# A hybrid decoder step: means of rows formed behind a half's first job, loads reordered, and weights times values in three passes of halves

## The chip, the cores and the metric

The kernel runs on one NeuronCore of a Trainium2 chip. The metric is the device time of one execution in microseconds (us); several executions are timed, and one is recorded by the hardware profiler. TensorE (PE) multiplies matrices, VectorE (DVE) and ScalarE (ACT) do elementwise work, GpSimd (POOL) helps, SyncE (SP) issues most DMAs. Each engine works off its own instructions in order and waits on semaphores for the others.

## The reference

One layer over T = 1104 token columns: 16 meta tokens and 1024 prompt tokens (causal), and 8 sequences of 8 sample tokens with 1024 cached positions each. The width is 1024, everything is float32.

```
x += 0.5 * rmsnorm(swiglu(rmsnorm(x, g1), Wg, Wu, Wd), g1p)        # FFN 1, hidden width 2816
h  = rmsnorm(x, gm); q, k, v, B, C, hc = split(h @ w_in)           # mixer
A  = softmax(q1 k1^T / 8) - lam * softmax(q2 k2^T / 8)             # 4 heads, two maps each
o  = rmsnorm(A @ v, subln) * (1 - lambda_init);  c = B * conv3(C * hc)
x += rmsnorm(concat(o, c) @ w_out, gp)
x += 0.5 * rmsnorm(swiglu(rmsnorm(x, g2), ...), g2p)               # FFN 2
rmsnorm(x, g) = x * rsqrt(mean(x * x) + eps) * g                   # mean over the 1024 features of a token
```

## The kernel before

Features lie on the 128 partitions, tokens in the columns. The 1104 columns are two **halves** p = 0, 1 of 552, each of two groups g of 276; a matmul takes 276 columns. Nearly every matrix product is made of float32r operands: each operand is split into a high part (ACT copies it, L175) and a low part (DVE subtracts, L176; the helper is `halves`), and `three` (L169 to L171) issues three passes, high x high, high x low, low x high.

The stages follow one another: `phase` for FFN 1's gate and up products, `down` for its down product, `phase` for w_in, attention, `down` for w_out, `phase` for FFN 2, `down` at the end.

**A phase.** Most of its weight units are done by `seven`: a unit is a 2 x 2 block product made with seven products instead of eight, of the operand's combinations that `quarters(p)` prepares (44 DVE operations and 28 ACT copies a half) and of the weights' combinations that `weights_piece(0..6)` prepares (DVE and ACT). Preparing takes time, so the first two or three jobs (unit u, half p) of a phase are **plain**: full float32 matmuls (L296) straight from the normalized rows in Y, 32 matmuls recorded as 64, over 8 chunks c of 128 features. Job (0,0) goes chunk by chunk with four PSUM banks, the others go group by group. `weights_of` loads a unit's raw weights into WR; one further unit per phase is copied early into a DRAM tile (`early`) and loaded from there into the end of W (`late_raw`).

**Between stages.** `down` sums tiles (q, dd, g) into Y, adds their squares into R (`sq_add`), and at the end of a half runs a background generator, `junction(p)`: `ready` forms the mean over features (`mean_r`: a matmul with a matrix of 1/1024, L204, then `rsqrt` on ACT and DVE), then per chunk multiplies by R and a gain (L543), adds the residual (L546) and stores the chunk; `heads` squares the chunk for the next norm into the tile ss2 (L218, L221, L222) and scales it by the next gain (L266), and after the last chunk it calls `mean_r` for the next norm; then `quarters`. For half 1 that is done in two parts, group 0 and group 1. The first layer's input goes through `heads` directly. A `Background` object steps through these generators between matmul jobs; `need(("h", p))` steps until that half's heads are done, the mean included, before a plain job of that half is written.

**Attention.** For each of 4 heads and 9 row blocks qi: `scores` (L929, float32r), `weights` (softmax and difference), `flip`: transposes of up to four 128 x 128 blocks into the one PSUM bank "fl" (L967), a copy to the tile "at" by DVE (L969) or ACT (L970) in turn, then the products with the values, one full float32 matmul per block (L982, recorded as two), and `sub_norm`. The sample sequences' work is spread between. Constants (identity, masks) lie in WR.

**Order.** `in_turn` writes a PE instruction behind the last one; a planner places everything else on each engine by its own simulated times, within the dependencies. `tc.issue_after(x)` puts what is written in it behind x on x's engine. `dma` issues from SP, `keep` from POOL.

Of the kernel before, what the change touches and what calls it, by code (L numbers as in the profile page):

```python
# [9 lines left out]
F32R = mybir.dt.float32r  # L10
# [5 lines left out]
P = 128  # L16
# [27 lines left out]
def hybrid_step(ctx: ExitStack, tc: tile.TileContext, ins, outs, n_pool):  # L44
# [104 lines left out]

    last_pe, last_dma = [None], [None]  # L150

# [104 lines left out]

    def heads(p, ready, gain, parts=((0, 1),)):


        ss2 = temp("ss2", HT)  # L260
        for gs in parts:
            t = slice(gs[0] * G, gs[-1] * G + G)
            for n, c in enumerate(ready(gs)):
                x = lay["yv"][p][:, c, :]
                sq_add(ss2, x, n == 0, gs)
                act.activation(x[:, t], x[:, t], AF.Copy, scale=gains[:, gain, c:c + 1])  # L266
                yield
            yield
            mean_r(lay["R"][p], ss2, gs)
            yield  # L270

    class Background:
# [15 lines left out]
    def plain(u, p, raw, use, outer, step):  # L288
# [11 lines left out]
        if outer:  # L300
            banks.update({(n, g): bank("mm")[:, :G] for g in range(2) for n in range(2)})
            for n, c in enumerate(PAIR_K):
                in_turn(part, [c], range(2))
                if n:
                    step()
                    if n > 2:
                        step()
            for g in range(2):
                use.plain(g, banks[0, g], banks[1, g])
        else:  # L310
            for g in range(2):
                banks.update({(n, g): bank("mm")[:, :G] for n in range(2)})
                for i in range(0, 8, 2):
                    in_turn(part, PAIR_K[i:i + 2], [g])
                    step()
                use.plain(g, banks[0, g], banks[1, g])

    def weights_of(src):
        dma(wraw, src)

    def weights_piece(n):
# [24 lines left out]
    def phase(n, src, early, late, uses, background, loaded=False, tail=iter(())):  # L346
# [6 lines left out]
        if not loaded:  # L353
            weights_of(src(1 - late))
        dma(late_raw, early)
        for u, p in [(0, 0), (0, 1), (1, 0)][:2 + late]:
            background.need(("h", p))
            if p and not late:
                for m in range(5):
                    weights_piece(m)  # L360
            plain(u, p, raws[u], uses(u, p), p == 0 and u == 0, background.step)
        if late:
            seven([(2, 0), (2, 1), (1, 1)] + [(u, p) for u in range(3, n) for p in range(2)], src, uses, background,
                  tail=tail)
        else:
            seven([(u, p) for u in range(1, n) for p in range(2)], src, uses, background, 5, tail)
# [110 lines left out]

    def down(src, blocks, base, order, place, w_src, reuse, g_post, g_pre, res, dst):

# [10 lines left out]
        inputs = [(p, b, i) for p in range(2) for b in range(nb) for i in range(blocks[b])]  # L490
        wt, raws, put = {}, [], []

# [19 lines left out]
        def load_input():  # L512
            p, b, i = inputs.pop(0)
            slot = xs[p][:, base(b) + i]
            dma(f32(slot[:, 0, :]), src(b, i, p))
            put.append(slot)

# [38 lines left out]
        def begin():  # L556
# [82 lines left out]
    for c in PAIR_K:  # L639
        dma(lay["yv"][1][:, c, :], ins["x1"][:, c, :])  # L640
    background = Background((("h", 0), heads(0, lambda gs: entering(0), G_F1PRE)),
                            (("h", 1), heads(1, lambda gs: entering(1), G_F1PRE)),
                            (("x", 0), quarters(0)), (("x", 1), quarters(1)))
# [178 lines left out]
    Q = [ring("q0", 4, TP, F32R), None]  # L822
    vs = ring("vs0", 1, 1152)
    qs_t, = ring("qs", 1, 1024)
# [12 lines left out]
    Q[1] = ring("q1", 4, TP, F32R)  # L837
    vbuf = [v.rearrange("p (j e) -> p j e", j=9) for v in vs + ring("vs1", 1, 1152)]
    pbuf = ring("p", 6, TP)
    abuf = [a.rearrange("p (j q) -> p j q", j=9) for a in ring("at", 4, 1152)]  # L840
    tq = ring("t", 10, 256)
    onesV, = ring("onesV", 1, P)
    cst = WR[:, 1470:]
    gp.memset(onesV, 1.0 / DV)
# [6 lines left out]

    dma(cst, ins["consts"])

# [8 lines left out]
    def load_v(h):  # L862
        dma(vbuf[h % 2][:, 0:8, :], v_spill[h, :, 0:8, :])
        dma(vbuf[h % 2][:N_META, 8, :], v_spill[h, :N_META, 8, :])
# [5 lines left out]
    load_v(0)  # L870
    for n in range(2):
        split_qk(0, n)

    def mixer_constants():
# [33 lines left out]
    def prompt_jobs(h):  # L908
# [50 lines left out]
        def flip(aw, qi):  # L959
            rows = N_META if qi == 0 else P  # L960
            at = of(abuf, "at")
            for j0 in range(0, qi + 1, 4):
                js = range(j0, min(j0 + 4, qi + 1))
                ps = bank("fl")
                for j in js:
                    kr = N_META if j == qi else P
                    nc.tensor.transpose(ps[:kr, (j - j0) * P:(j - j0) * P + rows], aw[:rows, j * P:j * P + kr],  # L967
                                        ident[:rows, :rows])
                copy = lambda dst, src: (dve.tensor_copy(dst, src) if (qi + j0 // 4) % 2  # L969
                                         else act.activation(dst, src, AF.Copy))  # L970
                n = len(js) - (js[-1] == qi)
                if n:
                    copy(at[:, j0:j0 + n, :rows], ps[:, :n * P].rearrange("p (j q) -> p j q", q=P)[:, :, :rows])
                if js[-1] == qi:
                    copy(at[:N_META, qi, :rows], ps[:N_META, n * P:n * P + rows])
            if qi < 1 or qi % 2 == 0:
# [139 lines left out]
    for step, job in enumerate(jobs):  # L1116
        nxt = step // 9 + 1
        if nxt < H:
# [21 lines left out]
    def place(p, b, q):  # L1140
        if q == 0:
# [3 lines left out]
    begin, run = down(both, (4, 4), lambda b: 4 * b, lambda p, b: (1, 2, 3, 0) if p and not b else (0, 1, 2, 3), place,  # L1145
                      lambda b, q: ins["w_out"][b, q], True, G_MPOST, G_F2PRE, x_spill, x_mid)
    for _ in begin:
# [94 lines left out]
```

## Time and profile before

| | us |
|---|---|
| median of 3 timed runs | 2297.01 (2293.79 to 2299.85) |
| the profiled execution | 2293.83 |
| its span | 2292.1 |
| PE busy | 2136.1 (93%) |
| DVE busy | 1404.7 (61%) |
| ACT busy | 929.5 (41%) |
| POOL busy | 299.8 (13%) |
| PE waiting for a mean's squares (L204 for ss) | 77.0 in 6 waits |

The profiled execution is 1.7 us longer than its span, and near the lowest of the timed runs. A busy engine is one with an instruction in flight; a matmul's record is longer than its spacing to the next one, so PE also counts as busy in short pauses. "Granted clock" is the share of TensorE's full 2.4 GHz that the chip gave; it has two levels, 1 and 0.5. The stages, by their times in the span: FFN 1 until about 802, w_in until 1106, attention until 1346, w_out until 1482, FFN 2 until the end.

### The profile page before, as it was taken

What the parts mean: (1) busy time and instruction counts of PE and PEld (TensorE: products, weight loads), DVE (VectorE), ACT (ScalarE), POOL (GpSimd) and SP (SyncE); (2) the same over time, 40 slices, a digit from 0 to 9 for tenths busy, and PEclk for the clock granted to TensorE, in tenths of its full rate; (3) what the DMA queues carried; (4) which work ended last, traced back from release to release, by engine and by line L of the source; (5) the groups of instructions that cost most, each with busy time, mean ns of one, the idle gap of its engine ahead of it and who ended that gap; (6) DMA issues with size and microseconds to landing.
All of it is one profiled execution on the core that took longest, in us unless ns stands there. A gap on an engine that the chain in (4) does not pass through costs nothing.

```text
span 2292.1 us, 41517 instructions
## 1 busy us (share of the span) xinstructions
PE 2136.1 (93%) x16126; PEld 2038.4 (89%) x16126; DVE 1404.7 (61%) x2973; ACT 929.5 (41%) x1960; POOL 299.8 (13%) x419
## 2 busy tenths in 40 slices
PE   6899999999999979999799978749999999999997
PEld 5799999999999959999667768739999999999997
DVE  5766556655567775466457656765665665645756
ACT  7433333334254442333235555553333333332522
POOL 0111111110000004443302110001111111100000
PEclk9899999999999989999789889879999999999998
DMA  7121222235444313321567332112122222543443
GB/s 276 55 81 67 81 81 68 81 116 197 130 144 142 131 51 120 124 86 60 191 206 274 125 137 102 67 35 78 67 81 81 68 80 81 175 144 127 141 148 98
DMA packets 115240, 263.48 MB, mean 115 GB/s; under 512 B 14514, under 2 KB 56114, under 8 KB 107602
## 3 DMA queue, kind: packets, MB, share of 16 engines
q1 hardware_dynamic: 109698, 244.92, 31.7%
q0 software_dynamic: 5344, 15.90, 1.9%
q8 instruction: 126, 2.06, 0.4%
q14 instruction: 72, 0.59, 0.1%
HBM read 206.47 MB, written 61.97 MB: 117 GB/s over the span
## 4 chain that ended last, share of the span: by engine, by line
PE 51%; issue 31%; DVE 7%; POOL 5%; DMA 3%; ACT 2%; SPq 1%; POOLq 0%; ACTq 0%; DVEq 0%
PE mm L169 13%; PE mm L170 13%; PE mm L171 13%; POOL u L440 3%; POOL n L440 3%; PE po L982 2%; PE mm L296 2%; PE qk L929 2%; DVE X L176 2%; PE fl L967 1%; PE sa L1059 1%; PE st L204 1%; PE sa L1024 1%; DVE Y L546 1%; DVE Y L543 1%
## 5 line engine op out<-in xcount | busy, mean ns | idle before, releaser
L169 PE MATMUL mm<-X,W 128*128 128x276 f32 x3868 | 1130.1, 292 | 27.8 <-ACT W L175 10.5
L170 PE MATMUL mm<-X,W 128*128 128x276 f32 x3868 | 1127.2, 291 | 2.8 <-DVE X L176 2.8
L171 PE MATMUL mm<-X,W 128*128 128x276 f32 x3868 | 1126.6, 291 | 1.9 <-DVE W L176 1.9
L169 PEld LDWEIGHTS mm<-X,W 128*128 128x128 f32 x3868 | 732.0, 189 | 31.0 <-ACT W L175 11.4
L170 PEld LDWEIGHTS mm<-X,W 128*128 128x128 f32 x3868 | 733.0, 190 | 4.3 <-DVE X L176 4.0
L171 PEld LDWEIGHTS mm<-X,W 128*128 128x128 f32 x3868 | 733.3, 190 | 3.2 <-DVE W L176 3.2
L176 DVE TENSOR_TENSOR W<-WR,W 128x512 fp32r<-128x512 f32 (+3 forms) x421 | 329.1, 793 | 116.4 <-ACT W L175 114.8
L175 ACT ACTIVATE W<-WR 128x512 fp32r<-128x512 f32 (+3 forms) x421 | 284.1, 689 | 249.6 <-PE mm L170 134.8
L420 ACT ACTIVATE n<-mm 128x276 f32<-128x276 f32 x210 | 84.2, 401 | 317.5 <-PE mm L171 299.0
L586 DVE TENSOR_TENSOR Y<-Y,mm 128x276 f32<-128x276 f32 x288 | 126.3, 439 | 128.1 <-PE mm L171 123.4
L440 POOL TENSOR_TENSOR u<-u,R 128x276 f32<-128x276 f32 x93 | 75.1, 807 | 493.2 <-ACT u L471 265.3
L440 POOL TENSOR_TENSOR n<-n,R 128x276 f32<-128x276 f32 x83 | 65.4, 787 | 547.2 <-ACT n L449 547.2
L170 PE MATMUL mm<-X 128*128 128x276 f32 x416 | 121.9, 293 | 2.7 <-DVE X L176 2.7
L169 PE MATMUL mm<-X 128*128 128x276 f32 x416 | 123.0, 296 | 1.5 <-ACT X L175 1.5
L423 DVE TENSOR_TENSOR n<-mm,n 128x276 f32<-128x276 f32 x105 | 46.8, 445 | 125.7 <-PE mm L171 113.9
L171 PE MATMUL mm<-X 128*128 128x276 f32 x416 | 121.4, 292 | 0.0
L221 ACT ACTIVATE sq<-Y 128x276 f32<-128x276 f32 x168 | 68.2, 428 | 86.4 <-DVE Y L586 58.7
L176 DVE TENSOR_TENSOR X<-X 128x552 fp32r<-128x552 f32 x104 | 75.5, 728 | 38.4 <-ACT X L175 37.9
L169 PE MATMUL mm<-X,X 128*128 128x276 f32 x320 | 93.9, 293 | 0.0
L170 PE MATMUL mm<-X,X 128*128 128x276 f32 x320 | 93.1, 291 | 0.0
L171 PE MATMUL mm<-X,X 128*128 128x276 f32 x320 | 93.1, 291 | 0.0
L929 PE MATMUL qk<-q,q 64*128 64x336 f32 (+10 forms) x360 | 69.9, 385 | 15.5 <-ACT q L175 11.1
(174 smaller groups left out, 2669.3 us busy)
## 6 DMA issues: line engine op xcount, KB each, us to landing
WR<-in_w_gu SPq DMA_DIRECT2D x43, 1024.0 KB, 4.8
WR<-in_w_dn SPq DMA_DIRECT2D x48, 640.0 KB, 3.9
X<-hid SPq DMA_DIRECT2D x88, 276.0 KB, 4.1
kp<-in_cache_k SPq DMA_DIRECT2D x64, 256.0 KB, 3.9
vp<-in_cache_v SPq DMA_DIRECT2D x64, 256.0 KB, 4.4
hid<-u SPq DMA_DIRECT2D x93, 138.0 KB, 1.8
hid<-n SPq DMA_DIRECT2D x83, 138.0 KB, 1.7
WR<-in_w_in SPq DMA_DIRECT2D x11, 1024.0 KB, 4.9
```

The lines of the kernel that those rows point to most:

```text
L169: nc.tensor.matmul(ps, lh, rh, start=first, stop=False, **kw)
L170: nc.tensor.matmul(ps, lh, rl, start=False, stop=False, **kw)
L171: last_pe[0] = nc.tensor.matmul(ps, ll, rh, start=False, stop=last, **kw).ins
L175: tc.keep_in_program_order(act.activation(hi, raw, AF.Copy))
L176: on.tensor_tensor(lo, raw, f32(hi), op=ALU.subtract)
L221: act.activation(sq, src[:, s], AF.Square)
L296: last_pe[0] = nc.tensor.matmul(banks[n, g], w, lay["yv"][p][:, c, g * G:g * G + G], start=c == PAIR_K[0], stop=c == PAIR_K[-1]).ins
L420: act.activation(t, ps, AF.Copy)
L423: dve.tensor_tensor(self.n1, ps, self.n1, op=ALU.add)
L440: on.tensor_tensor(t, t, lay["R"][p][:, g * G:g * G + G], op=ALU.mult)
L586: dve.tensor_tensor(y, y, ps, op=ALU.add)
L929: last_pe[0] = nc.tensor.matmul(pw[m], a[r, q0:q0 + P], b[r, k0:k1], start=n == 0, stop=n == 2, tile_position=(m * DH, 0)).ins
```

## The change

1. `heads` no longer calls `mean_r`, and yields twice less per part; it leaves its sums in `sums_of[p]`. A new `rms(p, gs)` forms that mean. `plain` calls it after the job's matmuls and before their results are used: for job (0,0) after all of them, for the others after each group. For half 0 of a `down`, `rms(0, (0, 1))` stands after tile 7 of half 1's last block. For the first input the sums are kept in R itself.
2. In the last block of half 1 the junction of half 1 steps from tile 9 on (tile 8 before), twice at tile 15; in w_out the junction of half 0 steps 8 times in block 0 (10 before).
3. A plain job steps its background only until what the next job needs is done (`upto`).
4. In FFN 1 the third plain job is written behind the load and the first five pieces of the next unit's weights; they were prepared after it. The load of `early` is written behind the last load noted in `last_load`.
5. `down` for w_out gets its first weight tile ready made (`have`): loaded in attention's step 4, split in step 12. Its inputs are split before its other weights.
6. In attention V is split into halves (`split_v`), the transposed weights are copied to a high part by ACT, the low part is subtracted by DVE, and `three` does the products. The constants get a tile of their own (cst) instead of a part of WR, loaded after the first V.

```diff
+    sums_of = {}
+    def rms(p, gs):
+        if p in sums_of:
+            mean_r(lay["R"][p], sums_of[p], gs)
+            if gs[-1]:
+                del sums_of[p]
-    def heads(p, ready, gain, parts=((0, 1),)):
-        ss2 = temp("ss2", HT)
+    def heads(p, ready, gain, parts=((0, 1),), at_r=False):
+        ss2 = sums_of[p] = lay["R"][p] if at_r else temp("ss2", HT)
...
                 yield
-            yield
-            mean_r(lay["R"][p], ss2, gs)
-            yield
...
+        def upto(self, name):
+            return lambda: self.step() if any(n == name for n, _ in self.named) else None
...
                     if n > 2:
                         step()
+            rms(p, (0, 1))
             for g in range(2):
                 use.plain(g, banks[0, g], banks[1, g])
...
                     step()
+                rms(p, (g,))
                 use.plain(g, banks[0, g], banks[1, g])
...
-        dma(late_raw, early)
-        for u, p in [(0, 0), (0, 1), (1, 0)][:2 + late]:
+        with tc.issue_after(last_load[0]):
+            dma(late_raw, early)
+        jobs = [(0, 0), (0, 1), (1, 0)][:2 + late]
+        for u, p in jobs:
             background.need(("h", p))
-            if p and not late:
+            if (u, p) == jobs[-1]:
+                if late:
+                    weights_of(src(2))
                 for m in range(5):
                     weights_piece(m)
-            plain(u, p, raws[u], uses(u, p), p == 0 and u == 0, background.step)
+            last = ("x", 1) if (u, p) == jobs[-1] else ("x", 0) if p else ("h", 1)
+            plain(u, p, raws[u], uses(u, p), p == 0 and u == 0, background.upto(last))
...
-            for n in range(max(blocks[0], 3)):
-                if n < 3:
+            if have:
+                for n in range(blocks[0]):
+                    split_input()
+            for n in range(3):
+                if n or not have:
                     split_item()
                     load_item()
-                if n < blocks[0]:
+                if not have:
                     split_input()
...
-                        if n % 4 == 3 if nb > 2 else n % 2 if b else n < 10:
+                        if n % 4 == 3 if nb > 2 else n % 2 if b else n < 8:
                             first.step()
-                        if p and b == nb - 1 and g:
+                        if p and b == nb - 1 and n > 8:
                             second.step()
+                            if n == 15:
+                                second.step()
                         if p and b == nb - 1 and n == 7:
+                            rms(0, (0, 1))
                             second = Background(*junction(1))
...
-    cst = WR[:, 1470:]
+    cst, = ring("cst", 1, K_W)
...
+    def split_v(h):
+        lo, hi = vbuf[h % 2]
+        halves(hi[:, 0:8, :], lo[:, 0:8, :], f32(lo[:, 0:8, :]), dve)
+        halves(hi[:N_META, 8, :], lo[:N_META, 8, :], f32(lo[:N_META, 8, :]), dve)
...
-                copy = lambda dst, src: (dve.tensor_copy(dst, src) if (qi + j0 // 4) % 2
-                                         else act.activation(dst, src, AF.Copy))
...
+                for src, r, j in parts:
+                    act.activation(hi[r, j, :rows], src, AF.Copy)
+                    dve.tensor_tensor(lo[r, j, :rows], src, f32(hi[r, j, :rows]), op=ALU.subtract)
...
-                nc.tensor.matmul(po[:, off:off + rows], vt_[:kr, j, :], at[:kr, j, :rows], start=j == 0, stop=j == qi)
+                three(po[:, off:off + rows], vt_[1][:kr, j, :], vt_[0][:kr, j, :], hi[:kr, j, :rows], lo[:kr, j, :rows],
+                      j == 0, j == qi)
...
+            if step % 9 == 7:
+                split_v(nxt)
+        if step == 4:
+            dma(WR[:, :1024], ins["w_out"][0, 0])
+        if step == 12:
+            w = W[:, 1024:2048], W[:, 0:1024]
+            halves(w[0], w[1], WR[:, :1024], dve)
+            first_w = {(0, 0, 0): (w[1], w[0])}
```

## Rows read from the trace of the kernel before

**Rows 1.** Page, part 1: each engine's busy us, share of the span, instructions.
```profile
PE 2136.1 (93%) x16126; PEld 2038.4 (89%) x16126; DVE 1404.7 (61%) x2973; ACT 929.5 (41%) x1960; POOL 299.8 (13%) x419
```

**Rows 2.** Waits of PE: who waited for whom, total us, times, longest.
```profile
PE st L204 <- DVE ss L222: 77.0, 6, 24.0
```

**Rows 3.** Timeline of PE: start, us, instructions, idle before and releaser.
```profile
17.39 2.18 PE L204 MATMUL st<-ss,onesD 128*128 128x276 f32 x4 [17.39 <-DVE ss L222]
...
74.75 0.60 PE L169 MATMUL mm<-X,W 128*128 128x276 f32 x1 [7.66 <-ACT W L175]
...
837.70 1.29 PE L204 MATMUL st<-ss,onesD 128*128 128x276 f32 x2 [11.18 <-DVE ss L222]
...
865.04 0.60 PE L169 MATMUL mm<-X,W 128*128 128x276 f32 x1 [6.25 <-ACT n L420]
...
1117.28 0.94 PE L929 MATMUL qk<-q,q 64*128 64x336 f32 x3 [11.09 <-ACT q L175]
...
1355.01 0.60 PE L169 MATMUL mm<-X,W 128*128 128x276 f32 x1 [8.60 <-ACT X L175]
...
1439.04 2.21 PE L204 MATMUL st<-ss,onesD 128*128 128x276 f32 x4 [12.72 <-DVE ss L222]
...
1530.80 1.29 PE L204 MATMUL st<-ss,onesD 128*128 128x276 f32 x2 [24.00 <-DVE ss L222]
```

**Rows 4.** Windows around the stage changes: us, each engine's busy time, clock, DMA.
```profile
18.00:39.00 21.00, 21.00 (x80) 16.76 (x79) 8.89 (x22) 17.99 (x40) 0.21 (x1) 1.00 1.02 350
39.00:87.00 48.00, 38.23 (x168) 31.86 (x167) 44.69 (x109) 26.49 (x72) 6.44 (x6) 0.86 0.16 57
795.00:866.00 71.00, 48.38 (x222) 40.03 (x222) 52.42 (x128) 34.43 (x84) 4.53 (x8) 0.84 0.14 49
1426.00:1441.00 15.00, 2.28 (x8) 1.60 (x6) 11.02 (x21) 8.80 (x20) 0.00 (x0) 0.62 0.21 79
1441.00:1552.00 111.00, 76.82 (x428) 68.63 (x427) 75.75 (x192) 60.50 (x145) 3.09 (x4) 0.82 0.14 47
```

**Rows 5.** Timeline of PE: a whole plain job of half 1, before w_in.
```profile
838.78 16.93 PE L296 MATMUL mm<-Y,W 128*128 128x276 f32 x64
```

**Rows 6.** Timelines of DVE and ACT before w_in's units.
```profile
811.05 0.44 DVE L222 TENSOR_TENSOR R<-R,sq 128x276 f32<-128x276 f32 x1
...
863.57 1.13 ACT L175 ACTIVATE W<-WR 128x512 fp32r<-128x512 f32 x2
864.61 0.67 ACT L420 ACTIVATE n<-mm 128x276 f32<-128x276 f32 x2
```

**Rows 7.** SP's issues and a window at attention's two ends.
```profile
1106.22 0.33 SPq L153 DMA_DIRECT2D W<-early_w  x1
...
1344.26 6.05 SPq L153 DMA_DIRECT2D WR<-in_w_out  x2
1350.41 1.79 SPq L153 DMA_DIRECT2D X<-c_spill  x4
...
1108.00:1116.00 8.00, 0.00 (x0) 0.00 (x0) 0.00 (x0) 1.00 (x1) 0.86 (x2) 0.55 0.94 341
```

**Rows 8.** Attention: a window, runs of matmuls, durations (min/median/max), DVE's copies.
```profile
1180.00:1346.00 166.00, 162.36 (x1340) 116.15 (x1340) 110.92 (x423) 89.34 (x237) 33.39 (x48) 0.95 0.52 173
...
1229.36 1.06 PE L982 MATMUL po<-at,vs 128*128 128x128 f32 x8
...
L982 PE MATMUL po<-at,vs x360: 257/275/579, 1137.1 to 1345.2; 128*128 128x128 f32 x144, 16*128 16x128 f32 x32, 16*128 16x16 f32 x4
...
1245.75 2.14 PE L1046 MATMUL sa<-s_comb,s_p 128*128 128x64 f32 x18
...
1228.88 0.44 PE L929 MATMUL qk<-q,q 64*128 64x144 f32 x2
...
L969 DVE COPY at<-fl 128x512 f32<-128x512 f32 x12 | 8.2, 683 | 0.4 <-PE fl L967 0.4
```

**Rows 9.** Timeline of PE: the last mean of the run.
```profile
2278.94 0.73 PE L204 MATMUL st<-R,onesD 128*128 128x276 f32 x2 [2.02 <-DVE R L222]
```

More of the change, by code (lines that the diff above doesn't have):

```diff
@@ L319, in weights_of @@
         dma(wraw, src)
+        last_load[0] = last_dma[0]
     def weights_piece(n):
@@ L354, in phase @@
             weights_of(src(1 - late))
-        dma(late_raw, early)
-        for u, p in [(0, 0), (0, 1), (1, 0)][:2 + late]:
+        with tc.issue_after(last_load[0]):
+            dma(late_raw, early)
+        jobs = [(0, 0), (0, 1), (1, 0)][:2 + late]
+        for u, p in jobs:
             background.need(("h", p))
-            if p and not late:
+            if (u, p) == jobs[-1]:
+                if late:
+                    weights_of(src(2))
                 for m in range(5):
                     weights_piece(m)
-            plain(u, p, raws[u], uses(u, p), p == 0 and u == 0, background.step)
+            last = ("x", 1) if (u, p) == jobs[-1] else ("x", 0) if p else ("h", 1)
+            plain(u, p, raws[u], uses(u, p), p == 0 and u == 0, background.upto(last))
         if late:
-            seven([(2, 0), (2, 1), (1, 1)] + [(u, p) for u in range(3, n) for p in range(2)], src, uses, background,
-                  tail=tail)
+            seven([(2, 0), (2, 1), (1, 1)] + [(u, p) for u in range(3, n) for p in range(2)], src, uses, background, 5,
+                  tail)
         else:
@@ L475, in plain, with down @@
             self.put(t, g)
-    def down(src, blocks, base, order, place, w_src, reuse, g_post, g_pre, res, dst):
+    def down(src, blocks, base, order, place, w_src, reuse, g_post, g_pre, res, dst, have=()):
         X, xs, yv, R = lay["X"], lay["xs"], lay["yv"], lay["R"]
@@ L490, in down @@
         inputs = [(p, b, i) for p in range(2) for b in range(nb) for i in range(blocks[b])]
-        wt, raws, put = {}, [], []
+        wt, raws, put = dict(have), [], []
+        loads = [n for n in loads if n not in wt]
         def key(p, b, q):
@@ L515, in load_input @@
             dma(f32(slot[:, 0, :]), src(b, i, p))
+            last_load[0] = last_dma[0]
             put.append(slot)
@@ L822, in hybrid_step @@
     Q = [ring("q0", 4, TP, F32R), None]
-    vs = ring("vs0", 1, 1152)
+    vs = ring("vs0", 1, 1152, F32R)
     qs_t, = ring("qs", 1, 1024)
@@ L837, in hybrid_step @@
     Q[1] = ring("q1", 4, TP, F32R)
-    vbuf = [v.rearrange("p (j e) -> p j e", j=9) for v in vs + ring("vs1", 1, 1152)]
+    vbuf = [[v.rearrange("p (j e) -> p j e", j=9) for v in (lo, hi)]
+            for lo, hi in (vs + ring("vh0", 1, 1152, F32R), ring("vs1", 2, 1152, F32R))]
+    cst, = ring("cst", 1, K_W)
     pbuf = ring("p", 6, TP)
-    abuf = [a.rearrange("p (j q) -> p j q", j=9) for a in ring("at", 4, 1152)]
+    abuf = [[a.rearrange("p (j q) -> p j q", j=9) for a in ring(f"at{n}", 2, 1152, F32R)] for n in range(2)]
     tq = ring("t", 10, 256)
     onesV, = ring("onesV", 1, P)
-    cst = WR[:, 1470:]
     gp.memset(onesV, 1.0 / DV)
@@ L862, in load_v @@
     def load_v(h):
[L863 to L864 removed]
+        lo = f32(vbuf[h % 2][0])
+        dma(lo[:, 0:8, :], v_spill[h, :, 0:8, :])
+        dma(lo[:N_META, 8, :], v_spill[h, :N_META, 8, :])
+    def split_v(h):
+        lo, hi = vbuf[h % 2]
+        halves(hi[:, 0:8, :], lo[:, 0:8, :], f32(lo[:, 0:8, :]), dve)
+        halves(hi[:N_META, 8, :], lo[:N_META, 8, :], f32(lo[:N_META, 8, :]), dve)
     load_qk(0)
@@ L870, in hybrid_step @@
     load_v(0)
+    dma(cst, ins["consts"])
     for n in range(2):
         split_qk(0, n)
+    split_v(0)
     def mixer_constants():
@@ L968, in flip @@
                                         ident[:rows, :rows])
-                copy = lambda dst, src: (dve.tensor_copy(dst, src) if (qi + j0 // 4) % 2
-                                         else act.activation(dst, src, AF.Copy))
                 n = len(js) - (js[-1] == qi)
+                parts = []
                 if n:
-                    copy(at[:, j0:j0 + n, :rows], ps[:, :n * P].rearrange("p (j q) -> p j q", q=P)[:, :, :rows])
+                    parts.append((ps[:, :n * P].rearrange("p (j q) -> p j q", q=P)[:, :, :rows], slice(0, P), slice(j0, j0 + n)))
                 if js[-1] == qi:
-                    copy(at[:N_META, qi, :rows], ps[:N_META, n * P:n * P + rows])
+                    parts.append((ps[:N_META, n * P:n * P + rows], slice(0, N_META), qi))
+                for src, r, j in parts:
+                    act.activation(hi[r, j, :rows], src, AF.Copy)
+                    dve.tensor_tensor(lo[r, j, :rows], src, f32(hi[r, j, :rows]), op=ALU.subtract)
             if qi < 1 or qi % 2 == 0:
@@ L1145, in hybrid_step @@
     begin, run = down(both, (4, 4), lambda b: 4 * b, lambda p, b: (1, 2, 3, 0) if p and not b else (0, 1, 2, 3), place,
-                      lambda b, q: ins["w_out"][b, q], True, G_MPOST, G_F2PRE, x_spill, x_mid)
+                      lambda b, q: ins["w_out"][b, q], True, G_MPOST, G_F2PRE, x_spill, x_mid, first_w)
     for _ in begin:
```

9 lines of the change are left out of this document (4 added, 5 removed).

## The prediction

> **What bounds the kernel now.** I read the page's busy shares first: TensorE is busy 93% of the span, VectorE 61%, ScalarE 41% [rows 1]. So the time is TensorE's work plus the places where it stands still, and the second view is who it waits for. One wait stands out: the mean's matmul (L204) waits for the squares' sum ss, 77.0 us in 6 waits [rows 2]. The third view, TensorE's timeline, shows where: 17.39 us at the start, 11.18 (and a smaller one) before w_in, 12.72 and 24.00 (and a smaller one) between w_out and FFN 2; beside them stand other pauses of 6 to 11 us at the same stage changes and at attention's two ends [rows 3]. The reader is to see that all of it lies at stage changes. There I asked for windows, to see what else could be late: VectorE is busy 8.89 of 21 us in the first stall, then 44.69 of 48 (93%); 52.42 of 71 (74%) before w_in; 11.02 of 15 and 75.75 of 111 (together 69%) before FFN 2 [rows 4]. So a wait taken from TensorE can be won back only as far as VectorE's own work there can be packed tighter. I use one rule for that: VectorE packs to 85%, halfway from the poorer windows to the 93% that the saturated one reaches; the bounds are no better than now (nothing won) and 92%.
>
> **Mean behind the job.** The mean's matmul stands in TensorE's order ahead of the plain job and holds it until the last chunk's square is added. After the change the job's 64 matmuls (16.93 us [rows 5]) stand ahead of the mean and need only their own chunk. The mean itself costs the same. What is late next is VectorE: behind the plain jobs come `seven`'s products, which need the quarters of half 1 and the weights' pieces. The trace shows that chain already: ScalarE's copy of a product (L420 at 864.61) stands behind the split of the weights (863.57) in its order, and TensorE waits 6.25 us for it [rows 3, 6].
>
> Start. VectorE's saturated stretch begins at 39, when the second half's mean is through; that mean stands on TensorE behind a job that began at 17.39 + 2. The job needs only the first of eight chunks that come in during the 17.39 us, and so can end up to half of that stall, 8 to 9 us, earlier (my estimate: the chunks arrive through all of it); the same VectorE work then begins earlier. By packing: 53.6 us of work between 18 and 87 [rows 4] at 85% is 63 instead of 69, 6 won; at 92%, 11; the wait of 7.66 before the products [rows 3] shrinks with it, and in FFN 1 the pieces are now made under the third job. I take 7 (0 to 13).
>
> Before w_in. 52.42 at 85% is 61.7 instead of 71: 9 won (0 to 14). What lets it pack: the half's post mean now needs only R, whose last sum is added at 811.05 [rows 6], and group 1's chain of chunks begins behind it and no longer behind the pre mean of group 0.
>
> Before FFN 2. 86.8 us of VectorE work in 126 [rows 4] at 85% is 102: 24 won (8 to 34). Here the 12.72 goes since the mean of half 0 moves from block 0 to tile 7 of block 1, and VectorE gets block 1's additions while it had little to do. The 24.00 goes since half 0's second job and half 1's group 0 stand ahead of that mean.
>
> **Loads.** At attention's start TensorE waits 11.09 us for the split of q [rows 3]. SP has issued `early` for FFN 2 (128 x 2048 floats, 1.05 MB) just ahead of q and k, and the DMAs move 341 GB/s between 1108 and 1116 [rows 7]: 1.05 MB is 3.1 us at that rate. Behind the last input of w_out it lies under w_out's products, which run from 1355. The constants move behind V on SP, 0.56 MB or 1.6 us at that rate, which may come off it. I take 3 won (0 to 4).
>
> At attention's end TensorE waits 8.60 us [rows 3]. SP stands on two loads of w_out's weights for 6.05 us, the second of which needs the place that the first is split from, and only then come the inputs (1350.41) [rows 7]. With the first tile ready and WR free of constants the inputs need not wait for attention's tail; what is left is their split. I take 11, the 8.60 and what the pauses and the lower clock behind it may give back (4 to 14).
>
> **Weights times values.** 360 records are 180 float32 products of two records each. A run of eight takes 1.06, and the last record is 0.275 long, so one record follows another by (1.06 - 0.275) / 7 = 0.112; 18 records of only 64 columns follow by (2.14 - 0.275) / 17 = 0.110 [rows 8]. So at these sizes the columns don't set the pace. Three passes at 0.112 are 0.336 instead of 0.224, and 180 x 0.112 = 20 us more on an engine that is busy 162 of 166 us there. Below: nothing, if three passes fit where two records were. Above: two float32r matmuls of 144 columns stand 0.44 - 0.27 = 0.17 apart [rows 8], though of an operand of 64 rows; at 0.17 it is 180 x (0.51 - 0.224) = 51 us. I take 20, by the nearer row (128 rows, 128 columns). The Trainium skill says something else of this price (TensorE: Matmul & The Clock Gate, section Back-to-back issue gap): a sustained stream of load and multiply pairs at 128 columns runs at about 81 ns each. By it three passes are 243 ns and the addition is only 3.4 us by my estimate, and the sum would be some 17 us lower; no row here shows a pair of 128 columns under 110 ns, so I don't use it.
>
> Beside it: 60 groups of transposes were copied once, half by each engine; now ScalarE copies and VectorE subtracts each. That is at most 30 x 0.68 = 20 us more on VectorE [rows 8] and 30 x 0.56 = 17 on ScalarE (half of the 1.13 for two pieces of 512 [rows 6]), and V's split adds 4 x 1152 columns, 6 and 5 us. VectorE is busy 111 of 166 us there, ScalarE 89 [rows 8], so I cost it at nothing; the cover is the scores of other blocks. If it is gone, the one "fl" bank is held 0.68 longer 60 times, 41 us.
>
> **Tail and rest.** At the end group 0's chain begins one tile later, and the last mean already waits 2.02 [rows 9]; one tile is 12 products, 1.5 us. I take 1 lost (0 to 2). The repeated means cost ScalarE table loads under stretches where it is half idle: nothing.
>
> **Sum.** 7 + 9 + 24 + 3 + 11 = 54 won, 20 + 1 lost: 33 us. Against the profiled execution, 2293.8 - 33 = 2260.8; the median of the runs lies 3.2 above that execution, so 2262 for a median, which allows for half of it.
>
> **Rivals.**
> *A, the stalls change their name.* VectorE and ScalarE keep the planner's order and pack hardly better than now: 1 + 3 + 14 + 2 + 8 = 28 won, 21 lost, about 2288. For it speaks the 6.25 us wait, which is of just this kind; against it that VectorE had 31% idle before FFN 2.
> *B, slower.* The products with the values: float32r passes of 128 columns cost as much as the two records of a float32 product, 0.224 a pass or near it, not one record. From 0.173 a pass the whole gain is gone (54 / 180 = 0.30 over 0.224, a third each). At 0.21 it is 180 x (0.63 - 0.224) = 73 us, and the time 2297 - 53 + 73 = 2317. For it speaks the 0.17 of the 144 column pair; against it the same pair, which by that price would stand 0.24 apart.
> *C, three passes for the price of two.* Passes come closer together than any record here (three in 0.224), or the added ones fill pauses too short for the profile to show as idle: 54 won, 1 lost, 2244. This is where the skill's figure above would lead.
> *D, everything packs.* VectorE reaches 92% everywhere and the loads give their upper ends: 13 + 14 + 34 + 4 + 14 = 79 won, 21 lost, 2239.
>
> **How the numbers follow.** Forecast 0.46, A 0.17, B 0.10, C 0.13, D 0.14. A change under 0.3% (7 us) can't be told from none. Forecast, C and D are faster (0.73); of A about half is, and a fifth of the half that isn't is slower; with B that gives faster 0.81, same 0.08, slower 0.11. The range 2230 to 2292 holds the forecast, C, D and most of A; its upper end is also the sum with passes at the price of 0.17 (2297 - 53 + 51). The forecast's own range is 2247 to 2277.
>
> **What would show it.** In the profile after: TensorE's waits for ss fall from 77 to under 15 us; the wait of 12.72 is gone and the plain jobs' runs break into chunks; VectorE's busy share over the last window (w_out's last blocks to FFN 2) rises to 80% or more; L420 and L175 take over what waits are left. Before attention the pause is near 8, behind it near 0. L982 has 540 records, 0.11 apart; attention from its first score to its last product is some 20 us longer. I am wrong if attention grows by 40 or more, if VectorE's share at the stage changes stays as it is, or if a new wait on loads stands before a plain job.

## The result, and the profile after

The change makes the kernel slower: 2364.98 us median (2362.32 to 2374.62, 4 runs) against 2295.40 (2288.08 to 2299.85, 4 runs) of the kernel before on the same chip, a ratio of 1.0314 with a 95% interval of 1.0274 to 1.0354. The forecast was 2262, with a range of 2230 to 2292. The profiled execution took 2364.88 us, its span is 2363.1, 71.0 longer than before.

The page of the kernel after, part 1 (engine, busy us, share, instructions), answers to [rows 1]:

```profile
PE 2218.3 (94%) x16306; PEld 2105.7 (89%) x16306; DVE 1429.9 (61%) x3025; ACT 953.3 (40%) x2013; POOL 295.7 (13%) x419
```

TensorE has 180 more records and is 82.2 us longer busy, 0.46 us a record, four times what a pass was priced at. Something besides the passes is in it.

PE's waits after (engine, line, waited for, total us, times, longest) answer to [rows 2]. The wait for ss, 77.0 us, is gone, in part by name only: all that the mean's matmul waits for falls from 82.7 (77.0, and 5.7 for R) to 20.3 (12.6 for R and 7.7 for sq). Other waits have come in its place:

```profile
PE mm L169 <- ACT n L437: 43.3, 3, 14.8
PE st L204 <- DVE R L222: 12.6, 3, 6.4
PE mm L305 <- DVE u L487: 12.0, 2, 11.3
PE st L204 <- DVE sq L200: 7.7, 2, 6.4
```

The timeline of PE after, at the stage changes (start, us, instructions, idle before and releaser), answers to [rows 3, 9]:

```profile
6.99 13.36 PE L305 MATMUL mm<-Y,WR 128*128 128x276 f32 x47 [6.99 <-DMA WR<-in_w_gu]
...
64.94 9.93 PE L305 MATMUL mm<-Y,W 128*128 128x276 f32 x32 [11.31 <-DVE u L487]
...
92.33 0.60 PE L169 MATMUL mm<-X,W 128*128 128x276 f32 x1 [14.39 <-ACT n L437]
...
768.58 0.60 PE L169 MATMUL mm<-X,W 128*128 128x276 f32 x1 [4.74 <-ACT X L175]
...
881.11 0.60 PE L169 MATMUL mm<-X,W 128*128 128x276 f32 x1 [14.84 <-ACT n L437]
...
1121.67 0.58 PE L962 MATMUL qk<-q,q 64*128 64x336 f32 x3
...
1443.29 0.60 PE L169 MATMUL mm<-X,W 128*128 128x276 f32 x1 [1.82 <-ACT X L175]
...
1565.12 1.29 PE L204 MATMUL st<-R,onesD 128*128 128x276 f32 x2 [6.38 <-DVE R L222]
...
1612.97 0.60 PE L169 MATMUL mm<-X,W 128*128 128x276 f32 x1 [14.04 <-ACT n L437]
...
2349.49 1.24 PE L204 MATMUL st<-R,onesD 128*128 128x276 f32 x2 [2.02 <-DVE R L222]
```

The 17.39 at the start became 6.99, and the first job ends 10 us earlier. But two new stalls follow, 11.31 and 14.39. The first takes the gain back: `seven`'s first pass comes at 74.50, and came at 74.75 before [rows 3]. The second is loss. Before w_in the 11.18 is gone, and the 6.25 became 14.84. Attention starts without a pause (11.09 before). Before FFN 2 the 24.00 is gone and a 14.04 came.

Laid side by side by the same numbered pass in both traces, the 71.0 us split so: FFN 1 up to its down +13.8, called the start below (10.4 of it by 123 us, and 2.7 about 545, in 6 us at half clock); FFN 1's down +8.8; before w_in -6.8 (with -0.2 in w_in); attention's start -11.2 (last pass of w_in to first score 11.4 before, 0.2 after); attention itself +90.5; its end and w_out's beginning -9.8; before FFN 2 -12.7 (-15.9 and +3.2); the rest -1.4. So 90.5 us stand against what the other parts moved, and nearly all of the experiments are about them.

Attention from its first score to its last product, in a window of each kernel (from:to, us; busy us and instructions of PE, PEld, DVE, ACT, POOL; granted clock; DMA share; GB/s). Before:

```profile
1117.28:1346.12 228.84, 217.15 (x1781) 155.03 (x1782) 145.21 (x547) 110.65 (x288) 44.43 (x74) 0.89 0.55 183
```

After, with two stretches of it:

```profile
1121.67:1441.03 319.36, 296.94 (x1963) 219.32 (x1962) 173.74 (x602) 131.71 (x337) 45.85 (x79) 0.71 0.43 141
...
1305.10:1339.20 34.10, 32.45 (x342) 24.58 (x334) 23.64 (x76) 16.95 (x42) 5.14 (x7) 1.00 0.63 201
1339.20:1369.90 30.70, 30.70 (x128) 22.20 (x126) 13.63 (x58) 11.93 (x34) 3.40 (x6) 0.50 0.08 27
```

The granted clock fell from 0.89 to 0.71. With levels of 1 and 0.5 that is 2 x 0.11 x 228.84 = 50 us at 1.2 GHz before and 2 x 0.29 x 319.36 = 185 after. In the last row TensorE has an instruction in flight for all of the 30.70 us, but starts 128, where the stretch ahead of it started 342: a full busy share hides the loss, the count and the clock show it.

The price of a pass held at full clock. Timeline of PE after:

```profile
1311.82 0.28 PE L169 MATMUL po<-at,vh 128*128 128x128 f32 x1
1311.93 0.27 PE L170 MATMUL po<-at,vh 128*128 128x128 f32 x1
1312.04 0.28 PE L171 MATMUL po<-at,vs 128*128 128x128 f32 x1
```

They start 0.11 apart, as the records of the float32 products did [rows 8]. At half clock the median spacing is 0.214, and 217 of the 540 passes ran there.

### The profile page after: what moved, and what is told of

Read it like the earlier page. It is cut to its first block, busy times and chain, and to the rows that moved or that the text cites. A ratio compares the mean times of both kernels' runs of the same rounds, so it can differ in the third digit from the quotient of the medians.

```text
span 2363.1 us, 41993 instructions
## 1 busy us (share of the span) xinstructions
PE 2218.3 (94%) x16306; PEld 2105.7 (89%) x16306; DVE 1429.9 (61%) x3025; ACT 953.3 (40%) x2013; POOL 295.7 (13%) x419
## 3 DMA queue, kind: packets, MB, share of 16 engines
HBM read 206.47 MB, written 61.97 MB: 114 GB/s over the span
## 4 chain that ended last, share of the span: by engine, by line
PE 36%; issue 17%; DVE 4%; POOL 3%; DMA 2%; ACT 1%; SPq 1%; POOLq 0%; DVEq 0%; ACTq 0%
PE mm L169 8%; PE mm L170 8%; PE mm L171 8%; PE qk L962 2%; POOL u L457 1%; PE po L169 1%; POOL n L457 1%; PE fl L1000 1%; PE po L170 1%; PE sa L1060 1%; PE po L171 1%; PE sa L1095 1%; DVE X L176 1%; DMA x_mid<-Y 1%; PE sa L1082 1%
## 5 line engine op out<-in xcount | busy, mean ns | idle before, releaser
L437 ACT ACTIVATE n<-mm 128x276 f32<-128x276 f32 x210 | 84.1, 401 | 314.7 <-PE mm L171 297.6
L305 PE MATMUL mm<-Y,W 128*128 128x276 f32 x320 | 82.2, 419 | 12.0 <-DVE u L487 11.3
```

What stands on the lines that cost most here:

```text
L305: last_pe[0] = nc.tensor.matmul(banks[n, g], w, lay["yv"][p][:, c, g * G:g * G + G], start=c == PAIR_K[0], stop=c == PAIR_K[-1]).ins
L437: act.activation(t, ps, AF.Copy)
```

## The experiments

All edits are to the changed kernel, unless said otherwise. The table gathers what the runs gave; "half" is 2 x (1 - clock) x length of attention's window. Single times come from one execution each; the kernel before ran between 2286 and 2300 in all batches.

| run | time, us | attention, us | clock | half, us |
|---|---|---|---|---|
| before | 2295.4 | 228.8 | 0.89 | 50 |
| after | 2365.0 | 319.4 | 0.71 | 185 |
| no_v | 2270.3 (4) | 229.3 | 0.91 | 41 |
| only_v | 2394.2 (4) | 325.0 | 0.67 | 215 |
| two_passes | 2357.6 | 313.3 | 0.67 | 207 |
| ballast | 2478.4 | 430.4 | 0.64 | 310 |
| copies_only | 2318.8 | 276.4 | 0.82 | 100 |
| passes_only | 2329.5 | 287.3 | 0.73 | 155 |
| wide_cols | 2294.2 | 247.6 | 0.91 | 45 |
| par_copies | 2324.3 | 276.7 | 0.81 | 105 |
| after_wide | 2337.2 | 291.4 | 0.83 | 99 |
| one_read | 2276.1 | 234.1 | 0.88 | 56 |
| start_means | 2275.8 | 233.1 | 0.90 | 47 |
| no_v_fix | 2254.6 (4) | 233.6 | 0.89 | 51 |
| all_dve | 2290.6 (10) | 268.4 | 0.88 | 64 |
| all_gp | 2319.9 | 297.5 | 0.78 | 131 |

**no_v: the change without its part on the values.** One copy of a group, in turn by DVE and ACT, and one float32 product, as before; V isn't split.

```diff
-  three(po[...], vt_[1][...], vt_[0][...], hi[...], lo[...], j == 0, j == qi)
+  nc.tensor.matmul(po[...], f32(vt_[0][...]), f32(lo[...]), start=j == 0, stop=j == qi)
```

> The changed kernel with the values' products as before (one full float32 product a block, one copy of the transposed weights); all other parts stay. If the three passes cost what attention's growth from 229 to 319 us (first score to last product) shows, the time falls by 85 to 95 us, to about 2275, below the kernel before. If the growth came from the moved constants or loads, attention stays above 280 us and the time above 2340.

Measured: ratio to before 0.9894 (0.9867 to 0.9922). Means and loads together win about 24 us (1%), though the start and FFN 1's down still lose 10.9 and 10.1 in this trace. Attention is back at 229.3. The two later runs with the same products (start_means, no_v_fix) have 233.1 and 233.6, so a difference of 4 us in attention says nothing.

**only_v: the kernel before with only the part on the values.**

> The kernel before with the values' products in three passes of halves and nothing else. If the passes alone do it: attention near 319 us, time 2295 + 80 to 95, about 2380. If it takes the other parts too: under 2330.

Measured: ratio 1.0472 (1.0418 to 1.0526); attention +96.2, while everything ahead of it adds up to 4.2 us. So the whole of attention's growth comes from this part, and no earlier transfer causes it.

**two_passes: without the pass of V's low half.** That part of the products is left out.

```diff
-  three(po[...], vt_[1][...], vt_[0][...], hi[...], lo[...], j == 0, j == qi)
+  nc.tensor.matmul(out, vt_[1][...], hi[...], start=j == 0, stop=False)
+  nc.tensor.matmul(out, vt_[1][...], lo[...], start=False, stop=j == qi)
```

> The changed kernel without the third pass (low part of V times high part of the weights is left out, so the products lose their last bits): as many records for the products as before, 360, but float32r ones. Clock theory (float32r passes of 128 columns keep the array too little at work, and the granted clock falls): the clock is still at half for more than 100 us of attention (49.6 before), attention over 270 us, time 2320 to 2350. Record theory (180 more records at their pace, and nothing else): attention back at about 235 us, time about 2280. Copy theory (copy and subtraction hold the one bank of transposes): attention hardly changes, time 2350 to 2375.

Measured: as many records as before (360), and attention still takes 313.3, with 207 us at half clock. The record theory falls. The time lies in the copy theory's band (2350 to 2375), attention and clock also in the clock theory's, so this run doesn't separate those two.

**ballast: one more float32 product a block, unused.**

> The changed kernel with one more full float32 product per block, into columns that are overwritten later (its result is used nowhere): 360 records more on TensorE, 40 us at the full clock. Clock theory: the added work keeps the clock up, half clock in attention falls from 184 us to under 100, and the time is no longer than 2375, maybe shorter than 2365. Record theory and copy theory: the work is simply added, attention grows by 40 us or more, time 2405 or more.

Measured: 2478.4, attention 430.4, clock 0.64. More work for TensorE did not hold the clock; that form of the theory fell. The 360 added records cost 111 us, 0.31 each.

**copies_only and passes_only: the part's two halves apart.**

```diff
 # copies_only
-  three(po[...], vt_[1][...], vt_[0][...], hi[...], lo[...], j == 0, j == qi)
+  nc.tensor.matmul(po[...], f32(vt_[1][...]), f32(lo[...]), start=j == 0, stop=j == qi)
 # passes_only
-  act.activation(hi[...], src, AF.Copy)
-  dve.tensor_tensor(lo[...], src, f32(hi[...]), op=ALU.subtract)
+  dve.tensor_copy(hi[...], src)  or  act.activation(hi[...], src, AF.Copy), in turn
-  three(..., hi[...], lo[...], ...)
+  three(..., hi[...], hi[...], ...)
```

> The changed kernel with both copies of the weights (ACT's rounded half, VectorE's subtraction) and the split of the values kept, and with one float32 product a block in place of the three passes (on the second halves, so that it waits for the whole copy chain; the first halves are left out of the product). Copy theory (the products come late because each bank of transposed weights is held for an ACT copy and then a subtraction, and PE's pauses bring the half clock): attention stays above 300 us with over 120 us at half clock, 2330 to 2375 us. Pass theory (the float32r passes themselves, 128 columns each, go with the half clock): attention falls back to 228 to 245 us with under 70 us at half clock, 2270 to 2295 us.

> The changed kernel with one copy of a group, taken in turn by VectorE and ACT as in the kernel before, and the three passes kept, all on that one rounded half (the low half of the weights is left out). Copy theory: attention falls to 228 to 250 us with under 70 us at half clock, 2270 to 2300 us. Pass theory: attention stays above 300 us with over 120 us at half clock, 2335 to 2375 us.

The attention windows of the two:

```profile
1116.90:1393.31 276.41, 237.83 (x1782) 170.80 (x1782) 173.16 (x602) 131.54 (x337) 44.70 (x79) 0.82 0.49 163
```

```profile
1117.44:1404.74 287.30, 273.34 (x1962) 208.91 (x1962) 154.42 (x558) 116.00 (x297) 48.12 (x79) 0.73 0.47 156
```

Neither theory's band was met. Against the 229.3 of no_v the copies alone cost 47.1 and the passes alone 58.0; both together cost 90.1, 15 less than the sum. There are two causes. The copies leave TensorE with no instruction for 38.6 of 276.4 us (16.7 in no_v); the other 25 of their 47 us are the same records taking longer, at a clock of 0.82. The passes leave TensorE busy (14.0 us without an instruction), at 0.73. Two of copies_only's waits in this window name the copy (total us, times, longest):

```profile
PE po L1017 <- DVE at L1010: 7.7, 7, 2.4
PE fl L1000 <- DVE at L1010: 6.0, 8, 1.7
```

In the first the products wait for the second copy, in the second the next transposes wait for the bank.

**wide_cols: passes_only with 28 of a head's 45 products widened to 256 columns.** The second 128 are not used.

```diff
+  w, x = (2 * P, hi[:, j:j + 2, :]) if j < qi - 1 else (rows, hi[:kr, j, :rows])
-  three(po[:, off:off + rows], ..., hi[...], hi[...], j == 0, j == qi)
+  three(po[:, off:off + w], ..., x, x, j == 0, j == qi)
```

> The run with the passes alone (one copy, three passes on the rounded half), with 28 of a head's 45 products widened from 128 to 256 moving columns (the second 128 are not used). Number of passes and order stay. If the passes go with the half clock because 128 columns leave TensorE little work for an instruction that takes 0.112 us anyway, a 256-column pass takes little longer at full clock (under 0.13 us), half clock in the attention falls from 155 to under 100 us and the attention from 287 to under 260 us: 2280 to 2305 us. If it is the number of passes, or their time, half clock stays above 130 us, the attention at 285 us or more: 2325 to 2375 us.

Its attention window, and three of the wide passes in PE's timeline:

```profile
1124.78:1372.35 247.57, 230.91 (x1962) 174.13 (x1962) 154.08 (x558) 115.95 (x297) 46.85 (x79) 0.91 0.56 183
```

```profile
1232.25 0.28 PE L169 MATMUL po<-at,vs 128*128 128x256 f32 x1
1232.36 0.28 PE L170 MATMUL po<-at,vs 128*128 128x256 f32 x1
1232.48 0.28 PE L171 MATMUL po<-at,vs 128*128 128x256 f32 x1
```

The same 1962 instructions with more columns in each run at a clock of 0.91 where they had 0.73; 39.7 us come back. A wide pass follows another by 0.115 in these rows, by 0.119 in the median at full clock. What remains over no_v is 18.3 us, the 20 that the prediction priced for 180 more passes.

**par_copies: copies_only with two copies that need nothing of each other.** The subtraction is left out.

```diff
-  dve.tensor_tensor(lo[...], src, f32(hi[...]), op=ALU.subtract)
+  dve.tensor_copy(lo[...], src)
```

> The run with the copies alone (ACT's half, VectorE's second read of the bank, one float32 product), with VectorE copying the bank instead of subtracting ACT's half from it, so that the two no longer follow each other (the subtraction is left out). If the chain of the two is what costs the 47 us of attention, it falls from 276 to 230 to 250 us and the time to 2270 to 2295 us. If it is the load of a second copy on VectorE (206.7 us busy there against 175.9), the attention stays at 265 to 280 us, 2305 to 2325 us.

Measured: nothing changed, 276.7, which is in the band of the load. The waits of DVE in attention (total us, times, longest), and then the timeline of ACT and DVE, say why it tells little:

```profile
DVE at L1010 <- ACT at L1009: 10.7, 17, 2.5
```

```profile
1249.61 0.60 ACT L1009 ACTIVATE at<-fl 128x512 fp32r<-128x512 f32 x1 [0.20 <-PE fl L1000]
...
1250.30 0.68 DVE L1010 CAST at<-fl 128x512 fp32r<-128x512 f32 x1
```

DVE still waits for ACT, though it uses none of ACT's result: in this program two engines' reads of one bank follow one another. The Trainium skill (PSUM — Partial Sum Buffer, section PSUM bank collisions raise a hardware error) says that ACT and DVE may not touch the same bank and partitions at once, reads included, so that a program has to order them; the 17 waits here agree. So this run did not take the chain away, and chain and load stayed unseparated.

**one_read: copies_only with the bank read once, and the other engine's copy taken from SBUF.** No low half is formed.

```diff
+  dve.tensor_copy(f32(lo[...]), src);   act.activation(hi[...], f32(lo[...]), AF.Copy)   # odd
+  act.activation(f32(lo[...]), src, AF.Copy);   dve.tensor_copy(hi[...], f32(lo[...]))   # even
```

> The run with the copies alone, with the bank of transposed weights read once, by VectorE and ACT in turn as in the kernel before, and the other engine's copy taken from SBUF; each engine still makes one copy of every group, and the float32 product waits for both (no low half is formed). If the 47 us come from a bank that two engines' queues hold, the attention falls from 276 to 230 to 250 us, 2270 to 2292 us. If they come from the two engines' load, or from the products that wait for both, it stays at 262 us or more, 2305 us or more.

```profile
1121.74:1355.83 234.09, 216.83 (x1782) 155.56 (x1782) 161.74 (x602) 129.24 (x337) 47.90 (x79) 0.88 0.59 192
```

```profile
PE fl L1000 <- DVE at L1010: 0.8, 2, 0.5
```

The same 602 DVE and 337 ACT instructions as in copies_only, and 42.3 of the 47.1 us are gone; of the two waits, 13.7 us together, under 2 are left. So the copies' price was the second engine's read of the one "fl" bank. The load as such is at most a small part of it: VectorE is busy 11.4 us less than in copies_only, but still 14.6 more than in no_v.

**after_wide: the changed kernel with wide passes.**

> The changed kernel itself, with 28 of a head's 45 products widened to 256 moving columns in all three passes (the second 128 are not used); copies, passes and their number stay. If the clock's part and the copies' part are separate, the attention falls from 319 us to about 276 + 18 = 294 us (285 to 300), half clock from 184 to 90 to 120 us, and the time to 2330 to 2345 us. If the copies alone are enough to keep the half clock with the passes there, the attention stays above 305 us and the time above 2350 us.

Measured: 2337.2 and 291.4 (294 expected), with 99 us at half clock. The two causes can be taken away one by one.

**start_means and no_v_fix: the losses outside attention.** start_means is no_v with the means of the first input back behind their heads. no_v_fix also undoes item 3's bound and item 4's order in FFN 1's first phase, and gives the heads of FFN 1's down their two empty steps back.

```diff
+  if at_r:
+      yield; rms(p, gs); yield
+  elif pad:              # FFN 1's down, half 0
+      yield; yield
...
-  if late: weights_of(src(2)); five pieces, ahead of the third job
-  plain(..., background.upto(last))
+  plain(..., background.step if late else background.upto(last))
```

> The run without the products' part, with the means of the first input alone back where they stood (behind each half's heads); the bound on the quarters and the earlier weight pieces stay as changed. If the means' place costs the start its 10 us, the time from the first seven-product job to FFN 1's down falls to that of the kernel before (within 2 us), 2255 to 2264 us. If the bound on the quarters does, the 14.4 us stall before the second such job stays and the time with it, 2264 to 2275 us.

> The changed kernel with values times weights as before (as in the run without the products' part), with the start's means and quarters in their old places, and with two empty steps behind the heads of the first half in FFN 1's down. If the start's and FFN 1's down's losses come from those places (13.8 and 9.5 us of the ledger), the start to the first down mean takes 668 to 672 us instead of 678, FFN 1's down falls by 8 to 10 us, the attention stays near 229 us, and the time is 2245 to 2262 us. If they come from the reordered loads (FFN 1's own weights and hidden inputs), it stays at 2265 to 2275 us.

start_means: the first pass comes at 66.1 (74.5 after), but TensorE then waits 16.44 us, the stall stays, and the start is 3.9 to 5.5 us slower than before's. The time of 2275.8 is just above the second band. That the means' place alone was the cause is wrong: of no_v's 10.9 half stays without it. With all three back, the start is level with before's (-1.2) and FFN 1's down too (+0.1). no_v_fix's ratio is 0.9839 (0.9817 to 0.9860): 1.6% faster than the kernel before, and faster than the changed one. It is the version to keep.

**all_dve and all_gp: no_v_fix with the three products, one read, and wide passes.** The bank goes to SBUF once; ACT rounds from there, and VectorE (or GpSimd) subtracts there.

> All parts of the change, correct products, with the bank of transposed weights read once (by VectorE and ACT in turn, into SBUF), the rounded half and the subtraction taken from SBUF by ACT and VectorE, 28 of a head's 45 products widened to 256 columns, and the start's and FFN 1's down's repairs. If the bank and the clock are the two causes, the attention takes 229 + 18 + 5 = 252 us (243 to 265) with under 80 us at half clock, and the time is 2254.6 + 18 + 5 = 2278 us (2265 to 2290). If the load of a third copy a group is a cost of its own, the attention stays above 275 us and the time above 2298 us.

> The same with the subtraction on GpSimd, which takes VectorE's added load away. If the two causes are all, 2265 to 2290 us as with VectorE; if GpSimd's subtractions are slow enough to hold the products, the attention is above 275 us and the time above 2298 us.

all_dve: ratio 0.9989 (0.9963 to 1.0016), attention 268.4, between the two bands, where 252 were expected, with the clock at 0.88. The two causes account for 51 of the 86 us that attention had over no_v_fix; 18.3 of the other 34.8 are the passes. Some 16 remain, with three copies a group (DVE's instructions 549 in no_v_fix, 642 here); whether it is their load was not tried. With the subtraction on GpSimd attention is longer, 297.5 us, at a clock of 0.78, as in the second band.

## Why the prediction was wrong

**Weights times values: priced +20, measured +90.5 in place.** The failed sentences are that the copies cost nothing, covered by other blocks' scores, and that passes stay at 0.112. The first: VectorE and ACT did have idle time [rows 8], but the cover that counts is the bank's, not the engine's. The prediction had named it, the one "fl" bank held 0.68 us longer 60 times, 41 us, and kept it only as the case of lost cover, outside its sum and its range (2262 + 41 is 2303). copies_only shows 47.1 for the copies alone; on top of the passes they cost 32.1 (90.1 - 58.0). The second: 0.11 a pass is right at full clock, and wide_cols shows 18.3 for it; but the price was taken from a stretch at 0.95 [rows 8], and with the passes alone attention ran at 0.73 and cost 58.0. The Trainium skill's 81 ns a pass (TensorE: Matmul & The Clock Gate, section Back-to-back issue gap) was rightly not used: at full clock the median spacing of the changed kernel's passes is 0.113, that of passes_only's 0.112.

**Rival B had the sign of the loss, not the mechanism.** Its 73 us are nearer to attention's 90.5 than the 20, but that is luck: 0.21 a pass is what passes cost at half clock; at full clock they do follow by one record's time, and B has no copies. Its time, 2317, is 48 below the measured one.

**Signs and sums.** Of the prediction's signs of being wrong, attention's growth came (90.5, where 40 was the limit), and a wait on a load stands before the first plain job, 6.99 us, though shorter than the 17.39 that stood there. VectorE's share before FFN 2 rose, but not to the 80% named. Three of its figures don't come out: by its own rule the bounds before FFN 2 are 0 and 32 (126 - 86.8 / 0.92), not 8 and 34, which rival D uses; and 2297 - 53 + 51 is 2295, not the range's end of 2292. None of them decides.

**Start: priced -7, measured +13.8.** The mean did move off the path (17.39 became 6.99). "The same VectorE work then begins earlier" failed. The timeline of ACT after:

```profile
60.68 1.28 ACT L191 ACT_TABLE_LOAD   x1
61.97 0.49 ACT L197 ACTIVATE sq<-st,eps_r 128x276 f32<-128x276 f32 x1
...
91.90 0.67 ACT L437 ACTIVATE n<-mm 128x276 f32<-128x276 f32 x2
```

The rsqrt of a mean that TensorE had made at 44.6 stands at 61.97, behind half 0's quarters and a table load; without R the job's banks aren't drained, and TensorE waits 11.31. L437, which drains the first seven-product bank, stands behind half 1's quarters; TensorE waits 14.39. With the means back the first stall goes and the second stays, 16.44 (start_means); with all back both go (no_v_fix). Item 3's bound lets the quarters come later, item 4 lets the weights' pieces come earlier; which of the two made the second stall was not separated.

**FFN 1's down: not priced, +8.8.** Item 1 takes two empty steps from the heads of half 0, and the background then runs two steps ahead. ScalarE's splits of FFN 1's hidden inputs (X<-X) before, and then after, with the quarters' copy (X<-n) ahead of the last:

```profile
732.42 0.65 ACT L175 ACTIVATE X<-X 128x552 fp32r<-128x552 f32 x1
...
734.14 0.65 ACT L175 ACTIVATE X<-X 128x552 fp32r<-128x552 f32 x1
...
737.90 0.66 ACT L175 ACTIVATE X<-X 128x552 fp32r<-128x552 f32 x1
```

```profile
745.00 0.65 ACT L175 ACTIVATE X<-X 128x552 fp32r<-128x552 f32 x1
...
752.89 0.65 ACT L175 ACTIVATE X<-X 128x552 fp32r<-128x552 f32 x1
...
760.91 0.65 ACT L175 ACTIVATE X<-X 128x552 fp32r<-128x552 f32 x1
...
767.53 0.43 ACT L175 ACTIVATE X<-n 128x276 fp32r<-128x276 f32 x1 [2.49 <-DVE n L249]
767.87 0.65 ACT L175 ACTIVATE X<-X 128x552 fp32r<-128x552 f32 x1
```

The first three splits of each list are the same ones. Before, they stand within 6 us; after, within 16, among half 0's quarters. The one behind them stands behind a quarters' copy that waits 2.49 us for VectorE, and TensorE waits 4.74 for it at 768.58. It isn't a wait for a load: that split is the fortieth of the 44, and the fortieth input was issued 40 us earlier, at 727.7. In no_v_fix, with the steps back, the three stand at 731.51, 733.23 and 734.95 again and the loss is gone; start_means, without the steps, still loses 10.2 there.

**Before w_in (-9) and before FFN 2 (-24): right in direction, -6.8 and -12.7.** Windows after at the stage changes answer to [rows 4]:

```profile
810.00:882.00 72.00, 53.00 (x282) 45.83 (x281) 57.98 (x141) 39.49 (x98) 4.53 (x8) 0.88 0.17 57
...
1507.00:1626.00 119.00, 86.02 (x491) 77.74 (x490) 91.95 (x222) 72.76 (x173) 3.81 (x5) 0.84 0.17 58
```

VectorE is at 81% and 77%, up from 74% and 69%, not at the 85% used. That share is the term that was too high: the prediction's own sums give 6 and 13 won with 81% and 77%. What is late instead is L437, as rival A said: -6.8 lies between A's 3 and the 9, and -12.7 just under A's 14.

**Loads: -14 priced, -21.0 measured** (-11.2 and -9.8). The end came out as worked out (11). At attention's start the whole pause went, where 3 us of transfer had been counted. SP's issue of q before, then after:

```profile
1106.71 0.33 SPq L153 DMA_DIRECT2D q<-q_spill  x1
```

```profile
1112.58 0.33 SPq L153 DMA_DIRECT2D q<-q_spill  x1
```

Before, `early` is issued 0.3 us after w_in's last pass (1105.90), and q right behind it; after, q is issued 8.9 us ahead of that pass (1121.45). Its split begins 8.3 us after the issue before (1115.00) and 4.0 after (1116.56): that is the transfer that was counted. The larger part is q's place in SP's order, behind a load that went out only at w_in's end.

**Tail: +1 priced;** the last wait is 2.02 as before [rows 9].

## What to carry to other kernels

Before a copy is split between two engines, ask how long the buffer that both read is held, and how many of that buffer there are: read it once, and let the second engine take it from the first one's copy. A matmul's price holds at the clock that it was read at; a new stream can run at another. Look at the count of instructions and the granted clock, since a busy share of 100% shows neither. Moving a wait from one engine's order moves the work behind it in the others' too: after such a move, look up what each in-order queue now has ahead of the instruction that frees a buffer.

## What the hardware showed that was not expected

Passes of 256 columns follow by 0.119 us (median, full clock) where those of 128 follow by 0.112, and with 28 of 45 products so widened the granted clock in attention rose from 0.73 to 0.91 and the time fell by 35 us (2329.5 to 2294.2, one execution each), though half of a wide pass's columns are thrown away. Adding float32 products to the 128-column passes did the opposite (0.71 to 0.64). What property of the stream the clock follows stays open.
